# Layer 0: the last two output tiles, the norm and the MLP's first contraction pair by token halves

## The chip, the cores and the metric

The kernel runs on one core of a Trainium2 chip. The metric is the device time of one execution in microseconds; the time before is the median of three runs. Engines are named as in the profile: PE is TensorE's matmuls and PEld its weight loads, DVE is VectorE, ACT ScalarE, POOL GpSimd, and SP the queue that issues the DMAs.

## What is computed

A trunk of two layers on 256 tokens of width 2048, in float32. The part that matters here, for each layer:

```python
mod = cond @ w_ada[l] + b_ada[l]
sh_a, sc_a, g_a, sh_m, sc_m, g_m = [m[:, None, :] for m in jnp.split(mod, 6, axis=-1)]
...
mix = jnp.concatenate([out_a, out_b], axis=-1) @ w_o[l]
x = x + g_a * mix

h = _rmsnorm(x) * (1.0 + sc_m) + sh_m
y = jnp.square(jax.nn.relu(h @ w_mlp_in[l])) @ w_mlp_out[l]
x = x + g_m * y
```

The norm needs the mean square over all 2048 features of a token, so it can't start for a token before the last output tile has been added to x for that token.

## The kernel before

Everything lies transposed: x is 16 tiles of 128 features (partitions) by 256 tokens. Each weight matrix is loaded as float32 (`raw`, five buffers that the modulation weights share) and split into two parts in a rounded format, `hi` by ScalarE (line 146) and `lo` by VectorE (line 147); four buffers of half a weight each hold hi, four hold lo. `mac` multiplies hi by the high part of the activations, hi by the low part, and lo by the high part: three TensorE passes (lines 182 to 184), each with a weight load of its own.

The attention's output product makes two tiles at a time. `pair` calls `tile_cols` for two weights, 16 feature tiles deep, so 48 passes for each tile; `update` (line 1006) adds the result times the gate to x, and `sumsq` squares it. The last two tiles (14 and 15) are squared apart (`sqa`, line 508). Then `rstd` takes the mean with a product in plain float32 (`pn`, line 526), a square root on ScalarE and a reciprocal on VectorE.

`norm_then_by_k` walks over eight pairs of feature tiles, pair 0 to 7. For each, `modulated` makes the two activations: ht on VectorE (line 604), the high part h on ScalarE (605), the low part on VectorE (606). `by_k` splits two weights of 128x1536 and runs 36 passes on each, 72 for a pair, into six PSUM banks (`pk`) that are open over all eight pairs. With these 12 tiles of the MLP begun, `mlp` goes on.

The modulation `mod` is made on VectorE: the weights w_ada come in loads of 1 MB (`ada`, issued on SP at line 289), and one instruction each multiplies by the condition and sums (line 297). There are 192 of them, in the order of need; shift and scale of the MLP come interleaved, four loads for two feature tiles of both. Two things set when a load is issued. Each weight that is split adds `rate` to a credit, and every full credit issues one load:

```python
self.credit += self.rate
while self.credit >= 1.0 and self.ada_todo:
    self.credit -= 1.0
    self.ada_load()
```

And `ada_need(l, g, i)` issues and sums at once, in a row, all that is still missing up to that column, before the work that follows. The rate is 1.1 for a weight in layer 0's output product (`RATE_A0`) and 0.6 in the pairs (`RATE_K`).

The engines' orders are fixed when the program is built. A scheduler sets them, except for PE where `manual_schedule` keeps the order of the code; in layer 0's output product and pairs that is not in force.

Of the kernel before, what the change touches and what calls it, by code (L numbers as in the profile page):

```python
# [10 lines left out]
F32 = mybir.dt.float32  # L11
F32R = mybir.dt.float32r
I32 = mybir.dt.int32
AF = mybir.ActivationFunctionType
ALU = mybir.AluOpType
AX = mybir.AxisListType

P = 128
T = 256
TX = T + 2  # L20
D = 2048
NK = D // P
# [72 lines left out]
NAHEAD = 6  # L95
NNORM = 12


RATE_A0, RATE_A1, RATE_A2, RATE_K, RATE_M = 1.1, 0.5, 0.7, 0.6, 0.66
# [3 lines left out]
class Trunk:  # L103
# [524 lines left out]
            out += self.split(t, "lat")  # L628
        return out

    def norm_then_by_k(self, l, acc, sh, sc, src, n, nwhole, fill=(), early=()):


        r = self.rstd(acc, D) if l or sh else acc
        banks = self.open_banks(2 * n)
        h = []
        for p in range(8):
            k = 2 * p
            for g in (sh, sc):
                self.ada_need(l, g, k + 1)  # L640
            whole = [] if p < nwhole else None
            h += self.modulated(r, k, self.mod[l, sh], self.mod[l, sc], whole)
            self.by_k(banks, [src[l, p, b] for b in range(2)], h, k, NK, 2 * n, whole)
            if fill:
                fill.pop(0)()
            if p in early:
                for g in (sh, sc):
                    self.ada_need(l, g, k + 3)
                early[p](h)
        return h, banks  # L650


    def layer(self, l, acc, st):
        nc, io = self.nc, self.io
# [4 lines left out]
        def next_by_k(kqs):  # L659
            def f(h):  # L660
                if not later:
                    later.extend(self.open_banks(2))
                for kq in kqs:
                    self.by_k(later, [io["w_d"][l, kq]], h, 4 * kq, NK)
            return f

        if l == 0:
            early = {p: next_by_k(kqs) for p, kqs in EARLY.items()}
            h, banks = self.norm_then_by_k(l, acc, 0, 1, io["w_a"], 3, WHOLE, self.fills(), early)
# [3 lines left out]
        else:  # L673
            h = acc
            lat = []
            for b in range(0, NAHEAD, 2):
                t, c = self.scaled(st, b, self.u("cr"))
# [7 lines left out]
        kk, qn, kn, qr, vm, a, at, v, o = [], [], [], [], [], [], [], [], []  # L685
# [108 lines left out]
        acc = None  # L794
        g = self.mod[l, 2]
        self.ada_need(l, 2, NK - 1)
        banks = self.open_banks(2)
# [6 lines left out]
        o = self.mo + o  # L804
        for kq in (2, 3):
            self.by_k(banks, [io["w_oa"][l, kq]], o, 4 * kq, NK)
        st = self.ahead(l, 3, 4, io["w_m0"][0]) if l else None
        for m in range(0, 4, 2):
            self.update(m, banks[m // 2], g)
            acc = self.sumsq(acc, self.x[:, m : m + 2])  # L810
        with self.tc.manual_schedule(engines={mybir.EngineType.PE}) if l else nullcontext():
            for m in range(4, NK, 2):
                self.update(m, self.pair([io["w_ob"][l, m - 4 + j] for j in range(2)], o), g)
                acc = self.sumsq(acc, self.x[:, m : m + 2], l == 0 and m == NK - 2)
                if st:
                    self.ahead_fill(st, 2 if m > 4 else 6)
            self.rate = RATE_K
            if st:
                h = self.ahead_rest(st, 0, acc, 2)
                first = NAHEAD, lambda: [self.relu2(*self.scaled(st, b, self.t("sum"))) for b in range(0, NAHEAD, 2)]  # L820
            else:
                h, banks = self.norm_then_by_k(l, acc, 3, 4, io["w_n0"], 3, 0)
                first = NNORM, lambda: [self.relu2(b) for b in banks]
        self.rate = RATE_M
        with self.tc.manual_schedule(engines={mybir.EngineType.PE}):
            return self.mlp(l, h, first, self.mod[l, 5])
# [437 lines left out]
```

## Time and profile before

| | |
|---|---|
| median of 3 runs | 2213.0 us (2212.81 to 2214.16) |
| profiled execution, its own time | 2214.89 us |
| its span | 2213.1 us |
| PE busy | 2167.0 us, 98% |
| DVE busy | 1613.2 us, 73% |
| ACT busy | 1158.8 us, 52% |
| sums of the modulation (line 297) | 192, 437.5 us |
| mean granted clock of TensorE | 0.991 |

A stretch of the profile reads: from and to, its length, the busy time of PE, PEld, DVE, ACT and POOL with their instructions, the granted clock, the DMA engines' share and GB/s. A row of the timeline has the start, the length, engine, line, tiles and shape; in brackets stands how long the engine had been idle and what released it. Lengths of matmuls overlap: the distance of two starts is what a pass takes from the engine. A waits row gives the sum, the number and the longest.

### The profile page before, as it was taken

How to read it: one execution, taken by the hardware profiler on the slowest of the kernel's cores; microseconds unless marked ns; L12 is line 12 of the kernel's file. 1: busy time of each engine (PE TensorE's matmuls, PEld its weight loads, DVE VectorE, ACT ScalarE, POOL GpSimd, SP SyncE). 2: the span in 40 equal slices, each digit the busy share in tenths (PEclk: the TensorE clock that was granted, in tenths of full speed). 3: DMA queues.
4: the chain of work that ended last, by engine and by line, in shares of the span. 5: the costliest groups of instructions: out<-in, count | busy, mean ns of one | idle time of the engine just before them, and what ended most of it. 6: DMA issues, size and time to landing. Idle time of an engine off the chain costs nothing.

```text
span 2213.1 us, 30961 instructions
## 1 busy us (share of the span) xinstructions
PE 2167.0 (98%) x12290; PEld 1907.8 (86%) x12290; DVE 1613.2 (73%) x2131; ACT 1158.8 (52%) x1722; POOL 25.5 (1%) x43
## 2 busy tenths in 40 slices
PE   7999999899999999999999999999999999999998
PEld 5898889898888888888888898999888888888886
DVE  8989778878778778777799876788544545555566
ACT  6555564446465355345455565647545534544544
POOL 0000000000000000000001000001000000000000
PEclk9999999999999999999999999999999999999999
DMA  9987678798888888888877766675554555555552
GB/s 391 404 332 298 241 276 320 283 339 335 308 318 327 311 307 321 330 307 303 339 253 293 259 243 228 235 287 202 197 198 176 204 195 174 190 207 183 188 202 94
DMA packets 85829, 586.44 MB, mean 265 GB/s; under 512 B 9522, under 2 KB 9906, under 8 KB 19634
## 3 DMA queue, kind: packets, MB, share of 16 engines
q1 hardware_dynamic: 85682, 584.46, 70.6%
q8 instruction: 96, 1.57, 0.3%
q14 instruction: 51, 0.41, 0.1%
HBM read 582.32 MB, written 2.10 MB: 264 GB/s over the span
## 4 chain that ended last, share of the span: by engine, by line
PE 90%; DVE 7%; ACT 2%; issue 1%; DMA 0%; SPq 0%; DVEq 0%; ACTq 0%
PE ps L203 21%; PE ps L206 11%; PE py L976 10%; PE py L974 10%; PE py L978 10%; DVE ada L297 4%; PE ps L184 2%; PE ps L182 2%; PE ps L183 2%; PE pk L184 2%; PE pk L182 2%; PE pk L183 2%; PE pv L253 1%; PE pv L254 1%; PE pv L255 1%; DVE lo L147 1%
## 5 line engine op out<-in xcount | busy, mean ns | idle before, releaser
L147 DVE TENSOR_TENSOR lo<-raw,hi 128x1024 fp32r<-128x1024 f32 (+1 forms) x720 | 850.8, 1194 | 480.4 <-ACT hi L146 322.5
L146 ACT ACTIVATE hi<-raw 128x1024 fp32r<-128x1024 f32 (+1 forms) x720 | 742.1, 1036 | 688.2 <-PE py L978 368.2
L203 PE MATMUL ps<-h,hi 128*128 128x512 f32 x2016 | 472.9, 391 | 0.0
L203 PEld LDWEIGHTS ps<-h,hi 128*128 128x128 f32 x2016 | 375.1, 188 | 75.8 <-DVE h L606 0.2
L297 DVE SCALAR_TENSOR_TENSOR ada<-ada,cond 128x2048 f32<-128x2048 f32 x192 | 437.5, 2284 | 0.7 <-DMA ada<-in_w_ada 0.5
L974 PE MATMUL py<-hi,hid 128*128 128x512 f32 x1024 | 326.5, 390 | 0.0
L976 PE MATMUL py<-lo,hid 128*128 128x512 f32 x1024 | 326.0, 389 | 0.0
L978 PE MATMUL py<-hi,hid 128*128 128x512 f32 x1024 | 325.7, 389 | 0.0
L206 PEld LDWEIGHTS ps<-h,lo 128*128 128x128 f32 x2016 | 250.5, 192 | 5.0
L206 PE MATMUL ps<-h,lo 128*128 128x256 f32 x2016 | 252.0, 283 | 0.0
L976 PEld LDWEIGHTS py<-lo,hid 128*128 128x128 f32 x1024 | 192.2, 188 | 40.7 <-DVE lo L147 0.7
L978 PEld LDWEIGHTS py<-hi,hid 128*128 128x128 f32 x1024 | 192.2, 188 | 40.0
L974 PEld LDWEIGHTS py<-hi,hid 128*128 128x128 f32 x1024 | 191.3, 188 | 38.8
L1012 ACT ACTIVATE sum<-ps 128x256 f32<-128x256 f32 x110 | 42.1, 383 | 110.4 <-PE ps L206 110.3
L182 PE MATMUL pk<-h,hi 128*128 128x256 f32 x304 | 87.8, 291 | 8.8 <-ACT h L605 5.8
L184 PE MATMUL pk<-h,lo 128*128 128x256 f32 x304 | 87.4, 289 | 1.1 <-DVE lo L147 1.1
L183 PE MATMUL pk<-h,hi 128*128 128x256 f32 x304 | 87.7, 289 | 0.0
L176 DVE TENSOR_TENSOR hid<-relu,hid 128x256 fp32r<-128x256 f32 x128 | 48.3, 420 | 47.5 <-ACT hid L175 47.5
L239 PE MATMUL pk<-hf,w 128*128 128x256 f32 x288 | 64.8, 385 | 9.0 <-ACT hf L610 8.9
L239 PEld LDWEIGHTS pk<-hf,w 128*128 128x128 f32 x288 | 55.5, 194 | 17.6 <-ACT hf L610 9.8
L182 PEld LDWEIGHTS pk<-h,hi 128*128 128x128 f32 x304 | 60.0, 198 | 9.9 <-ACT h L605 6.2
L184 PEld LDWEIGHTS pk<-h,lo 128*128 128x128 f32 x304 | 60.0, 198 | 1.5 <-DVE lo L147 1.5
(252 smaller groups left out, 2815.8 us busy)
## 6 DMA issues: line engine op xcount, KB each, us to landing
raw<-in_w_m SPq DMA_DIRECT2D x238, 1024.0 KB, 4.9
ada<-in_w_ada SPq DMA_DIRECT2D x192, 1024.0 KB, 5.0
raw<-in_w_ob SPq DMA_DIRECT2D x24, 1024.0 KB, 4.9
raw<-in_w_dv SPq DMA_DIRECT2D x16, 1024.0 KB, 4.8
raw<-in_w_q SPq DMA_DIRECT2D x16, 1024.0 KB, 5.0
raw<-in_w_n SPq DMA_DIRECT2D x16, 768.0 KB, 5.7
w<-in_w_a SPq DMA_DIRECT2D x24, 384.0 KB, 11.1
raw<-in_w_a SPq DMA_DIRECT2D x12, 768.0 KB, 6.4
```

The source lines that it names most:

```text
L146: nc.scalar.activation(hi, v, AF.Copy)
L147: ins = nc.vector.tensor_tensor(lo, v, hi.bitcast(F32), ALU.subtract)
L182: mm(ps, hi, x[0], start=first, stop=False, skip_group_check=shared)
L183: mm(ps, hi, x[1], start=False, stop=False, skip_group_check=shared)
L184: mm(ps, lo, x[0], start=False, stop=last, skip_group_check=shared)
L203: mm(ps.rearrange("p a b -> p (a b)"), part(w, 0, k), both, start=k == 0, stop=False)
L206: mm(ps[:, 0], part(w, 1, k), x, start=False, stop=k == nk - 1)
L239: self.nc.tensor.matmul(ps, w[i][:, j * P : j * P + P], whole[i], start=first, stop=last, skip_group_check=True)
L297: ins = nc.vector.scalar_tensor_tensor(w, w, 1.0, self.cond, ALU.mult, ALU.mult, accum_out=acc[:, i : i + 1])
L974: mm(o, xh[:, tok], hi[:, part[j]], start=start, stop=False)
L976: mm(o, xh[:, tok], lo[:, part[j]], start=False, stop=False)
L978: mm(o, xl[:, tok], hi[:, part[j]], start=False, stop=stop)
```

## The change

For layer 0 alone, output tiles 14 and 15, the norm and pair 0 are written out in `by_halves`, and PE keeps the order of the code there. Each product is made for tokens 0 to 127 and for tokens 128 to 255 apart, so the passes are 128 columns wide and there are twice as many, each with its weight load. The order on PE is: tile 14 first half, tile 15 first half, tile 14 second half, the mean of the first half, tile 15 second half, pair 0's first weight on the first half, the mean of the second half, the second weight on the first half, both weights on the second half. The updates, squares, root, reciprocal and h are made by halves too. From the weights of tile 12 on, the rate is 0, so that no modulation load is issued on credit until pair 1, where it is 0.6 again. Layer 1's code is only written in another order.

```diff
+    def by_halves(self, l, o, g, acc):
+        nc, io = self.nc, self.io
+        m = NK - 2
+        toks = [slice(t * P, t * P + P) for t in range(2)]
+        sh, sc = self.mod[l, 3], self.mod[l, 4]
+        for grp in (3, 4):
+            self.ada_need(l, grp, 1)
+        ps, pn = self.bank("ps"), self.bank("pn")[:, 0]
...
+        def out(j, tok):
+            for k in range(NK):
+                x = (o[k][0][:, tok], o[k][1][:, tok])
+                self.mac(ps[:, j, tok], ws[j][k // 8], (k % 8) * P, P, x, k == 0, k == NK - 1)
+
+        def squares(tok):
+            for i in range(2):
+                x = self.x[:, m + i, tok]
+                nc.vector.scalar_tensor_tensor(x, ps[:, i, tok], g[:, m + i : m + i + 1], x, ALU.mult, ALU.add)
+            sq = self.t("sqh")[:, :, :P]
+            nc.scalar.activation(sq, self.x[:, m : m + 2, tok], AF.Square)
+            return sq
+
+        def norm(sq, tok):
+            vals = [acc[0][:, tok], acc[1][:, tok], sq[:, 0], sq[:, 1]]
+            for i, v in enumerate(vals):
+                nc.tensor.matmul(pn[:, tok], self.mean[D], v, start=i == 0, stop=i == 3)
...
+        out(0, toks[0])
+        out(1, toks[0])
+        sq = squares(toks[0])
+        out(0, toks[1])
+        norm(sq, toks[0])
+        out(1, toks[1])
+        sq = squares(toks[1])
+        banks = self.open_banks(6)
...
+        into(0, toks[0])
+        norm(sq, toks[1])
+        into(1, toks[0])
+        into(0, toks[1])
+        into(1, toks[1])
+        return r, banks, h
...
-        for p in range(8):
+        for p in range(len(h) // 2, 8):
...
+        if l == 0:
+            for m in range(4, NK - 2, 2):
+                if m == NK - 4:
+                    self.rate = 0.0
+                self.update(m, self.pair([io["w_ob"][l, m - 4 + j] for j in range(2)], o), g)
+                acc = self.sumsq(acc, self.x[:, m : m + 2])
+            with self.tc.manual_schedule(engines={mybir.EngineType.PE}):
+                begun = self.by_halves(l, o, g, acc)
+            self.rate = RATE_K
+            h, banks = self.norm_then_by_k(l, None, 3, 4, io["w_n0"], 3, 0, begun=begun)
```

What that does to the built order shows at three places. First PE, at the end of the output product (ps is its PSUM bank, pn the mean's, pk the pair's; in brackets the engines whose semaphores the row waits for). Before:

```order
L183 MATMUL ps_3841<-do_3052,hi_3910 128x256
L184 MATMUL ps_3841<-do_3052,lo_3911 128x256
L526 MATMUL pn_3971<-sqa_3967,mean_117 128x256 [waits Activation_49]
L526 MATMUL pn_3971<-sqa_3969,mean_117 128x256 [waits Activation_49]
L182 MATMUL pk_3979<-h_3986,hi_3996 128x256 [waits Activation_49]
L182 MATMUL pk_3980<-h_3986,hi_3996 128x256
L182 MATMUL pk_3981<-h_3986,hi_3996 128x256
L183 MATMUL pk_3979<-h_3986,hi_3996 128x256 [waits DVE_49]
```

and now, where tile 15 of the first half is done and tile 14 of the second half begins:

```order
L183 MATMUL ps_3838<-do_3052,hi_3857 128x128
L184 MATMUL ps_3838<-do_3052,lo_3858 128x128
L182 MATMUL ps_3838<-moh_2463,hi_3843 128x128 [waits DVE_49]
L183 MATMUL ps_3838<-mol_2464,hi_3843 128x128
L184 MATMUL ps_3838<-moh_2463,lo_3844 128x128
L182 MATMUL ps_3838<-moh_2463,hi_3843 128x128
L183 MATMUL ps_3838<-mol_2464,hi_3843 128x128
L184 MATMUL ps_3838<-moh_2463,lo_3844 128x128
```

The wide passes with two waits for ScalarE's squares and one for h between them became narrow ones; the first pass of the second half waits for VectorE, for the update of x that reads the same bank.

Second the DMA queue, from pair 4's second weight on (raw is a weight, in_w_n a pair's and in_w_m the MLP's; ada is a modulation load). Before:

```order
L158 DMA raw_4465<-in_w_n 128x1536
L158 DMA raw_4522<-in_w_n 128x1536
L289 DMA ada_4532<-in_w_ada 128x2048
L158 DMA raw_4570<-in_w_n 128x1536
L158 DMA raw_4626<-in_w_n 128x1536
L289 DMA ada_4636<-in_w_ada 128x2048
L158 DMA raw_4674<-in_w_n 128x1536
L289 DMA ada_4686<-in_w_ada 128x2048
L158 DMA raw_4733<-in_w_n 128x1536
L158 DMA raw_4780<-in_w_n 128x1536
L289 DMA ada_4790<-in_w_ada 128x2048
L158 DMA raw_4832<-in_w_m 128x2048
```

and now, behind pair 5's second weight:

```order
L289 DMA ada_4746<-in_w_ada 128x2048
L289 DMA ada_4786<-in_w_ada 128x2048
L289 DMA ada_4789<-in_w_ada 128x2048
L158 DMA raw_4802<-in_w_n 128x1536
L158 DMA raw_4848<-in_w_n 128x1536
L289 DMA ada_4858<-in_w_ada 128x2048
L289 DMA ada_4897<-in_w_ada 128x2048
L289 DMA ada_4901<-in_w_ada 128x2048
L289 DMA ada_4904<-in_w_ada 128x2048
L158 DMA raw_4917<-in_w_n 128x1536
L289 DMA ada_4927<-in_w_ada 128x2048
L158 DMA raw_4965<-in_w_n 128x1536
```

Where single loads stood between the weights, three stand ahead of pair 6's two weights and four ahead of pair 7's first.

Third VectorE ahead of pair 7's h (macc and mod are the modulation's sums and results; ht and h are pair 7's). Before:

```order
L147 TENSOR_TENSOR lo_4677<-raw_4674,hi_4676 128x768
L147 TENSOR_TENSOR lo_4681<-raw_4674,hi_4680 128x768
L297 SCALAR_TENSOR_TENSOR ada_4636,macc_88<-ada_4636,cond 128x2048
L147 TENSOR_TENSOR lo_4736<-raw_4733,hi_4735 128x768
L307 SCALAR_TENSOR_TENSOR mod_87<-macc_88,vec 128x2
L604 SCALAR_TENSOR_TENSOR ht_4724<-x,mod_87,rstd_3976 128x256 x2
L147 TENSOR_TENSOR lo_4740<-raw_4733,hi_4739 128x768
L606 SCALAR_TENSOR_TENSOR h_4725<-ht_4724,mod_85,h_4725 128x256
L606 SCALAR_TENSOR_TENSOR h_4726<-ht_4724,mod_85,h_4726 128x256
```

and now:

```order
L147 TENSOR_TENSOR lo_4855<-raw_4848,hi_4854 128x768
L297 SCALAR_TENSOR_TENSOR ada_4858,macc_86<-ada_4858,cond 128x2048
L297 SCALAR_TENSOR_TENSOR ada_4897,macc_86<-ada_4897,cond 128x2048
L297 SCALAR_TENSOR_TENSOR ada_4901,macc_88<-ada_4901,cond 128x2048
L309 TENSOR_TENSOR mod_85<-macc_86,vec 128x2
L297 SCALAR_TENSOR_TENSOR ada_4904,macc_88<-ada_4904,cond 128x2048
L307 SCALAR_TENSOR_TENSOR mod_87<-macc_88,vec 128x2
L604 SCALAR_TENSOR_TENSOR ht_4908<-x,mod_87,rstd_3840 128x256 x2
L147 TENSOR_TENSOR lo_4920<-raw_4917,hi_4919 128x768
L606 SCALAR_TENSOR_TENSOR h_4909<-ht_4908,mod_85,h_4909 128x256
```

Four sums stand in a row between the last split of pair 6 and pair 7's ht, where one sum stood among the splits; ahead of pair 6's ht three sums stand in the same way.

More of the change, by code (lines that the diff above doesn't have):

```diff
@@ L629, in latent, with into @@
         return out
[L631 to L636, printed above, removed]
-        for p in range(8):
+    def by_halves(self, l, o, g, acc):
[6 more added lines that the diff above has]
+        ps, pn = self.bank("ps"), self.bank("pn")[:, 0]
+        r = self.cp.tile([P, T], F32, tag="rstd", name=self.name("rstd"), bufs=2)
+        ws = [self.weights(io["w_ob"][l, m - 4 + j]) for j in range(2)]
+        h = [self.parts("h") for _ in range(2)]
+        def out(j, tok):
[13 more added lines that the diff above has]
+                nc.tensor.matmul(pn[:, tok], self.mean[D], v, start=i == 0, stop=i == 3)
+            nc.scalar.activation(r[:, tok], pn[:, tok], AF.Sqrt, bias=self.eps)
+            nc.vector.reciprocal(r[:, tok], r[:, tok])
+            t = self.t("hth")
+            for i, (hi, lo, _) in enumerate(h):
+                nc.vector.scalar_tensor_tensor(t[:, i, tok], self.x[:, i, tok], sc[:, i : i + 1], r[:, tok], ALU.mult, ALU.mult)
+                nc.scalar.activation(hi[:, tok], t[:, i, tok], AF.Identity, bias=sh[:, i : i + 1])
+                nc.vector.scalar_tensor_tensor(
+                    lo[:, tok], t[:, i, tok], sh[:, i : i + 1], hi[:, tok].bitcast(F32), ALU.add, ALU.subtract
+                )
+        out(0, toks[0])
[6 more added lines that the diff above has]
+        banks = self.open_banks(6)
+        w = []
+        def into(b, tok):
+            for i, part in enumerate(w[b]):
+                for j in range(6):
+                    tile = 6 * b + j
+                    x = (h[i][0][:, tok], h[i][1][:, tok])
+                    first = i == 0 and tile % 2 == 0 and tok.start == 0
+                    self.mac(banks[tile // 2][:, tile % 2, tok], part, j * P, P, x, first, False, True)
+        for b in range(2):
+            w.append(self.weights(io["w_n0"][l, 0, b], 1536))
+        into(0, toks[0])
[4 more added lines that the diff above has]
+        return r, banks, h
@@ L638, in norm_then_by_k @@
+    def norm_then_by_k(self, l, acc, sh, sc, src, n, nwhole, fill=(), early=(), begun=None):
+        if begun:
+            r, banks, h = begun
+        else:
+            r, banks, h = acc, self.open_banks(2 * n), []
+        for p in range(len(h) // 2, 8):
             k = 2 * p
@@ L810, in layer @@
             acc = self.sumsq(acc, self.x[:, m : m + 2])
-        with self.tc.manual_schedule(engines={mybir.EngineType.PE}) if l else nullcontext():
-            for m in range(4, NK, 2):
+        if l == 0:
+            for m in range(4, NK - 2, 2):
+                if m == NK - 4:
+                    self.rate = 0.0
                 self.update(m, self.pair([io["w_ob"][l, m - 4 + j] for j in range(2)], o), g)
-                acc = self.sumsq(acc, self.x[:, m : m + 2], l == 0 and m == NK - 2)
-                if st:
+                acc = self.sumsq(acc, self.x[:, m : m + 2])
[3 more added lines that the diff above has]
+            h, banks = self.norm_then_by_k(l, None, 3, 4, io["w_n0"], 3, 0, begun=begun)
+            first = NNORM, lambda: [self.relu2(b) for b in banks]
+        else:
+            with self.tc.manual_schedule(engines={mybir.EngineType.PE}):
+                for m in range(4, NK, 2):
+                    self.update(m, self.pair([io["w_ob"][l, m - 4 + j] for j in range(2)], o), g)
+                    acc = self.sumsq(acc, self.x[:, m : m + 2])
                     self.ahead_fill(st, 2 if m > 4 else 6)
-            self.rate = RATE_K
-            if st:
+                self.rate = RATE_K
                 h = self.ahead_rest(st, 0, acc, 2)
[L820 to L823, printed above, removed]
+            first = NAHEAD, lambda: [self.relu2(*self.scaled(st, b, self.t("sum"))) for b in range(0, NAHEAD, 2)]
         self.rate = RATE_M
```

## The prediction

> **What bounds the kernel now.** I read the busy shares and the chain that ended last first, then stretches of ten microseconds around the changed place, then the waits of TensorE there.
>
> ```profile
> PE 2167.0 (98%) x12290; PEld 1907.8 (86%) x12290; DVE 1613.2 (73%) x2131; ACT 1158.8 (52%) x1722; POOL 25.5 (1%) x43
> PE 90%; DVE 7%; ACT 2%; issue 1%; DMA 0%; SPq 0%; DVEq 0%; ACTq 0%
> ...
> 410.00:420.00 10.00, 8.95 (x72) 8.64 (x70) 9.96 (x12) 1.64 (x3) 0.00 (x0) 1.00 0.86 323
> 420.00:430.00 10.00, 2.85 (x11) 2.04 (x11) 9.16 (x17) 3.97 (x8) 0.00 (x0) 0.68 0.89 308
> 430.00:440.00 10.00, 10.00 (x71) 10.00 (x71) 9.26 (x20) 6.47 (x13) 0.00 (x0) 0.80 0.33 120
> 440.00:450.00 10.00, 10.00 (x86) 10.00 (x85) 9.55 (x12) 4.00 (x5) 0.00 (x0) 1.00 0.77 277
> 490.00:500.00 10.00, 10.00 (x86) 10.00 (x85) 8.22 (x9) 7.34 (x14) 0.00 (x0) 1.00 1.00 378
> ...
> PE pk L182 <- ACT h L605: 5.8, 1, 5.8
> PE pn L526 <- ACT sqa L508: 2.4, 2, 2.0
> ```
>
> TensorE (the first busy number of a stretch) bounds nearly everything; from 440 us on it has no gap until the pairs end at 500. The seam between the output product and the MLP's first pair is the exception: two waits there sum to 8.2 us, and the granted clock (third number from the right) falls to 0.68 and 0.80. The seam pass by pass:
>
> ```profile
> 406.42 0.28 PE L182 MATMUL ps<-moh,hi 128*128 128x256 f32 x1
> ...
> 418.55 0.28 PE L183 MATMUL ps<-do,hi 128*128 128x256 f32 x1
> 418.67 0.28 PE L184 MATMUL ps<-do,lo 128*128 128x256 f32 x1
> 420.98 0.70 PE L526 MATMUL pn<-sqa,mean 128*128 128x256 f32 x2 [2.02 <-ACT sqa L508]
> 422.01 0.70 PE L526 MATMUL pn<-sqa,mean 128*128 128x256 f32 x2 [0.34 <-ACT sqa L508]
> 428.55 1.01 PE L182 MATMUL pk<-h,hi 128*128 128x256 f32 x3 [5.84 <-ACT h L605]
> 429.36 0.41 PE L183 MATMUL pk<-h,hi 128*128 128x256 f32 x1
> 429.57 0.41 PE L184 MATMUL pk<-h,lo 128*128 128x256 f32 x1
> ...
> 439.63 0.28 PE L182 MATMUL pk<-h,hi 128*128 128x256 f32 x1
> ```
>
> The first row opens output tile 14, the last opens contraction pair 1. So what the change rewrites takes 439.63 - 406.42 = 33.2 us now, for 96 + 72 = 168 passes. A pass of 256 tokens starts every 0.12 us at full clock (418.55 to 418.67) and every 0.21 us just after the gap (429.36 to 429.57). All the change can win lies in these 33.2 us: 168 x 0.12 = 20.2 is work, 8.2 waits, and the rest half clock and the norm's own products.
>
> **The change part by part.**
>
> *Half as wide, twice as many.* The 168 passes become 336 of 128 tokens, each with its own weight load. What does a 128-token pass cost? The trace has no such pass in this number format; the nearest rows:
>
> ```profile
> 500.27 7.28 PE ps L203 x32
> 507.55 3.83 PE ps L206 x32
> ...
> 40.15 0.28 PE L375 MATMUL pl<-vec,mean 128*128 128x4 f32 x2
> ...
> 40.15 0.19 PEld L375 LDWEIGHTS pl<-vec,mean 128*128 128x128 f32 x1
> 40.26 0.19 PEld L453 LDWEIGHTS pb<-oh,lsch 128*128 128x128 f32 x1
> 40.38 0.19 PEld L454 LDWEIGHTS pb<-oh,lscl 128*128 128x128 f32 x1
> ...
> 97.52 0.19 PEld L182 LDWEIGHTS pk<-h,hi 128*128 128x128 f32 x1 [0.99 <-ACT hi L146]
> 97.63 0.19 PEld L183 LDWEIGHTS pk<-h,hi 128*128 128x128 f32 x1
> ...
> 222.49 0.60 PE L1094 MATMUL pt<-ident,a 128*128 128x128 f32 x4
> ```
>
> The chain gives 7.28 / 32 = 0.2275 us for 512 columns and 3.83 / 32 = 0.12 for 256; along that line 128 columns would be 0.12 - 0.054 = 0.066. But a load stands before each pass. At 40.15 the passes have four columns, next to nothing, and still loads start 0.11 and 0.12 apart. At 97.52, after a wait, the second load starts 0.11 after the first. [...] I take 0.112, nearest the four-column rows; ends: 0.066, if short loads overlap better than any row shows, and 0.12. Then 336 x 0.112 = 37.6 us.
>
> [...]
>
> *The norm's products.* Four plain float32 matmuls, which the trace records as eight passes of 256 columns, become eight, so 16 passes of 128. The four transposes in the last row, of that width and format, start (0.60 - 0.28) / 3 = 0.11 apart, 0.28 being the length of one pass: 1.8 us.
>
> *A new wait.* The first pass of the second token half writes the PSUM bank that VectorE still reads for the residual update of the first half, and the built order makes it wait for that.
>
> ```profile
> 406.62 0.88 DVE L1006 SCALAR_TENSOR_TENSOR x<-ps,mod,x 128x256 f32<-128x256 f32 x2 [2.15 <-PE ps L184]
> 416.04 1.82 DVE L147 TENSOR_TENSOR lo<-raw,hi 128x768 fp32r<-128x768 f32 x2
> 423.60 1.75 DVE L533 RECIPROCAL rstd<-rstd 128x256 f32<-128x256 f32 x1
> 425.26 2.23 DVE L297 SCALAR_TENSOR_TENSOR ada<-ada,cond 128x2048 f32<-128x2048 f32 x1
> 427.42 1.27 DVE L604 SCALAR_TENSOR_TENSOR ht<-x,mod,rstd 128x256 f32<-128x256 f32 x3
> 428.61 1.27 DVE L606 SCALAR_TENSOR_TENSOR h<-ht,mod,h 128x256 fp32r<-128x256 f32 x3
> ...
> 412.93 1.58 ACT L146 ACTIVATE hi<-raw 128x768 fp32r<-128x768 f32 x2 [2.88 <-DMA raw<-in_w_n]
> ```
>
> Two updates of half width lie between 0.45 and 0.88 us; with the end of the last pass (0.28, less one pitch) and the hand-over I take 0.9. Behind it queue all later passes. The rest of the norm is covered: after the half's mean product, split 0.9, reciprocal 0.9 (half of 1.75), four half-width steps and two on ScalarE make some 3.5 us, against 48 x 0.112 = 5.4 us of the other tile; the second half's some 3 us lie beside 36 x 0.112 = 4.0. If a pass took 0.066, that second cover (2.4) would be gone.
>
> So the stretch becomes 37.6 + 1.8 + 0.9 = 40.3 us instead of 33.2: **+7.1**. The 8.2 us of waits and the half clock do go; the loads eat more than that. Ends: +6.5 at 0.110, +9.8 at 0.12, -8.3 at 0.066.
>
> *The postponed modulation loads.* Five load-and-sum steps move from the seam behind it. On SP they leave slots to the weights; nothing there is scarce, since PE never waits for a DMA in this stretch. But pair p needs columns 2p and 2p+1 of scale and shift, four sums, and the rate gives 1.2 per pair. Before, the lead sufficed to pair 7. Now it runs out: in VectorE's order three sums stand in a row ahead of pair 6's h and four ahead of pair 7's, where one stood in each place. No sum is added in all, but here they are on the path. From the rows: a sum 2.2 (425.26 to 427.42), a split of a half weight 0.91, an ht or h step 0.40, a split on ScalarE 0.79; a pair on TensorE 72 x 0.12 = 8.6.
>
> VectorE can split pair 4's last half weight when TensorE leaves pair 3, since the buffers hold four halves. From the start of pair 4: 1.8 for both engines' splits and their hand-over, 2.2 sum, 0.9, 0.8, 0.9, 0.8 for pair 5's splits and h, 2.2 sum: 9.6, which is 1.0 after pair 5 began. Then two splits (2.8), three sums (9.4), three splits, two ht and an h (13.3). Pair 5 ends at 8.6: TensorE waits **4.7 us**. Then an h, a split, four sums, two ht, a split, an h: 12.2 more, at 25.5; pair 6 ended at 13.3 + 8.6 = 21.9: **3.6 us**. Together 8.2 (25.5 against two pairs).
>
> Such waits also cost clock:
>
> ```profile
> 208.60:211.30 2.70, 0.00 (x0) 0.00 (x0) 1.96 (x10) 2.04 (x5) 0.00 (x0) 1.00 0.91 373
> 212.10:218.90 6.80, 6.23 (x26) 5.43 (x25) 5.83 (x13) 3.57 (x9) 0.00 (x0) 0.50 0.45 172
> ...
> 1161.10:1164.00 2.90, 0.02 (x1) 0.03 (x1) 2.90 (x7) 2.17 (x5) 0.74 (x2) 1.00 0.33 136
> 1164.40:1167.80 3.40, 3.40 (x18) 3.40 (x17) 3.40 (x6) 0.46 (x1) 0.00 (x0) 0.50 0.60 169
> ```
>
> Waits of 2.7 and 2.9 us brought half clock for 6.8 and 3.4 us. At 0.21 instead of 0.12, 3.4 us at half clock lose 1.5 us. The loss after the first wait is hidden, since pair 7 starts when VectorE lets it; after the second it is 1.5 to 3.0, and I take 2. So **+10.2**; ends 5 (some sums finish while the half weights are still in hand) and 14 (loads land late too: DMA stood at 0.77 to 1.00 of its time in pairs 1 to 7, and seven 1 MB loads now crowd into two pairs).
>
> Sum: 7.1 + 10.2 = 17.3. Against the profiled execution's own 2214.9 that is 2232.2; the median of the three runs stands 1.9 lower, so I forecast 2213.0 + 17.3, rounded to **2230 us**.
>
> **The rivals.**
> - *A short pass is priced by its columns* (0.066). For: the two chain rows lie on a line. Against: loads 0.11 apart under four-column passes. The stretch shrinks by 8.3, the forced sums stay: 2213.0 - 8.3 + 10.2 = 2214.9, not slower within what a measurement can tell. It decides below 0.074 per pass (30.5 - 10.2 + 4.4 over 336); below 0.06 the kernel would be faster. [...] Chance 0.13.
> - *The forced sums stay hidden*: VectorE takes them while it waits for weight slots. For: it is only 73% busy in all. Against: its order is fixed, and its stretches here are 8 to 9.6 us busy of 10. Then 2213.0 + 7.1 = 2220. Chance 0.08.
> - *Narrow passes lose the fast format* and run like plain float32, whose 128-column records take 0.11, two to a matmul: 0.22. Then 336 x 0.22 = 73.9, the stretch grows by 43, and the time is about 2266. Nothing in the trace shows it. Chance 0.06.
>
> **How the numbers follow.** The forecast case has 0.67; its own range is 2225 to 2236 (passes 0.110 to 0.12, sums 6 to 13). The rivals have 0.27, and 0.06 is left for what I don't see, half of it faster. A measurement of this kernel tells about 0.2%, 4.4 us, from no change. Faster: 0.02 of the first rival and 0.03, 0.05. Same: 0.06 of the first rival and 0.01, 0.07. Slower: 0.88. The range 2216 to 2238 takes in the second rival and the slower half of the first, and leaves out the third, the fast half and the tails.
>
> **What would show it.** In the profile after: the starts of 128-token passes 0.11 to 0.12 apart, with a load interval as long; no wait of PE for h or sqa left; one wait of about 0.9 us for the residual update; two waits of TensorE of 3 to 5 us ahead of pairs 6 and 7, with sums just before on VectorE, and half clock behind each. The prediction is wrong if passes start 0.07 apart, or if no wait stands ahead of pairs 6 and 7.

## Result: 27 us slower, ten more than forecast

| kernel | median, us | runs | ratio to before, 95% interval |
|---|---|---|---|
| before | 2213.3 (2212.8 to 2214.2) | 4 | |
| after | 2240.5 (2237.1 to 2244.6) | 4 | 1.0123 [1.0111, 1.0135] |

The sign was right; the time lies 10.5 us above the forecast of 2230 and 2.5 us above the range. The four executions fall in two groups, 2244.6 and 2243.8, and 2237.1 and 2237.3. The profiled one is that of 2244.6 us (span 2242.8; before 2214.9 and 2213.1), so the trace has 29.7 us to explain. Where passes open, in after less before:

| place in TensorE's order | after, us | later than before, us |
|---|---|---|
| output tile 14 | 406.36 | -0.1 |
| contraction pair 1 | 459.55 | 19.9 |
| pair 5 | 494.14 | 20.0 |
| pair 6 | 506.61 | 23.8 |
| pair 7 | 519.17 | 27.7 |
| the MLP's second product | 551.23 | 28.9 |
| end | 2242.81 | 29.7 |

Twenty microseconds are lost in the rewritten seam, 9.0 more from pair 1 to the second product, 0.8 in layer 1. In pairs 1 to 4 nothing is lost: the 9.0 begin with the wait ahead of pair 6.

The rewritten seam in stretches; the granted clock is the third number from the right, DMA's share the second:

```profile
406.40:412.00 5.60, 5.60 (x53) 5.60 (x52) 2.70 (x4) 1.61 (x2) 0.00 (x0) 1.00 0.52 180
420.40:430.00 9.60, 9.60 (x47) 9.60 (x47) 3.44 (x5) 2.18 (x4) 0.00 (x0) 0.50 0.10 26
430.00:440.00 10.00, 10.00 (x49) 10.00 (x49) 3.21 (x7) 2.62 (x5) 0.00 (x0) 0.50 0.13 53
440.00:447.60 7.60, 7.60 (x38) 7.60 (x37) 0.00 (x0) 0.00 (x0) 0.00 (x0) 0.50 0.42 140
447.70:455.00 7.30, 7.30 (x68) 7.30 (x67) 6.90 (x18) 4.07 (x10) 0.00 (x0) 1.00 0.00 0
```

TensorE has work throughout: busy time fills every stretch. But it does 53 passes in 5.6 us in the first, and 49 in 10 us in the third, where the clock is 0.50. The half clock lasts from 420.35 to 447.65, 27.3 us. Its passes, its beginning and its end:

```profile
416.81 0.28 PE L183 MATMUL ps<-do,hi 128*128 128x128 f32 x1
416.92 0.28 PE L184 MATMUL ps<-do,lo 128*128 128x128 f32 x1
417.89 0.33 PE L182 MATMUL ps<-moh,hi 128*128 128x128 f32 x1 [0.70 <-DVE x L652]
418.06 0.28 PE L183 MATMUL ps<-mol,hi 128*128 128x128 f32 x1
...
425.56 0.41 PE L183 MATMUL ps<-do,hi 128*128 128x128 f32 x1
425.77 0.41 PE L184 MATMUL ps<-do,lo 128*128 128x128 f32 x1
425.99 1.16 PE L660 MATMUL pn<-acc,mean 128*128 128x128 f32 x4
...
448.05 0.27 PE L184 MATMUL pk<-h,lo 128*128 128x128 f32 x1
448.16 0.27 PE L182 MATMUL pk<-h,hi 128*128 128x128 f32 x1
```

At full clock a narrow pass starts every 0.11 us (416.81 to 416.92, and again at 448.05), at half clock every 0.21 (425.56 to 425.77). The only idle time of TensorE in the whole seam is the 0.70 us ahead of 417.89, the wait for VectorE's residual update; the clock falls 2.5 us behind it. It comes back only after the second set of norm products (pn).

TensorE's waits in the whole trace, those that changed (line, releaser: us in total, times, longest):

```profile
PE pa L184 <- DVE lo L147: 6.0, 3, 4.9
PE pk L182 <- ACT h L605: 4.7, 2, 3.7
PE ps L182 <- DVE x L652: 0.7, 1, 0.7
```

The first row was 4.3 us before, its longest 2.9; it stands at the start of layer 1, where the last 0.8 us are lost. The waits for h and sqa in the seam are gone (5.8 and 2.4 us before). The two for h that are left stand ahead of pairs 6 and 7, and half clock follows the first of them only (505.68 to 512.51):

```profile
506.61 0.80 PE L182 MATMUL pk<-h,hi 128*128 128x256 f32 x2 [3.66 <-ACT h L605]
...
519.17 0.62 PE L182 MATMUL pk<-h,hi 128*128 128x256 f32 x3 [1.08 <-ACT h L605]
```

And the loads' place in the DMA engines, from stretches of 20 us, before and then after:

```profile
420.00:440.00 20.00, 12.85 (x80) 12.04 (x81) 18.43 (x36) 10.44 (x21) 0.00 (x0) 0.74 0.61 214
```

```profile
420.00:440.00 20.00, 20.00 (x98) 20.00 (x97) 6.65 (x11) 4.80 (x8) 0.00 (x0) 0.51 0.12 40
...
500.00:520.00 20.00, 15.05 (x100) 14.44 (x98) 19.93 (x28) 6.30 (x10) 0.00 (x0) 0.83 1.01 395
```

What was transferred at 0.61 of DMA's time in the seam is transferred at pairs 6 and 7, where DMA stands at 1.01, that is, all of its time.

### The profile page after: what moved, and what is told of

It reads as the page before. It is cut to its first block, busy times and chain, and to the rows that moved or that the text cites. A ratio compares the mean times of both kernels' runs of the same rounds, so it can differ in the third digit from the quotient of the medians.

```text
span 2242.8 us, 31313 instructions
## 1 busy us (share of the span) xinstructions
PE 2197.7 (98%) x12466; PEld 1940.2 (87%) x12466; DVE 1613.4 (72%) x2138; ACT 1160.8 (52%) x1725; POOL 22.6 (1%) x43
## 4 chain that ended last, share of the span: by engine, by line
PE 78%; DVE 3%; issue 0%; ACT 0%; DVEq 0%; ACTq 0%
PE ps L203 20%; PE ps L206 11%; PE py L1051 10%; PE py L1053 10%; PE py L1049 10%; PE ps L182 1%; PE ps L184 1%; PE ps L183 1%; PE pk L183 1%; PE pk L184 1%; PE pk L182 1%; PE pa L184 1%; PE pa L183 1%; PE pa L182 1%; DVE ada L297 1%; PE pv L255 1%
## 5 line engine op out<-in xcount | busy, mean ns | idle before, releaser
L182 PE MATMUL pk<-h,hi 128*128 128x256 f32 (+1 forms) x328 | 95.7, 296 | 7.7 <-ACT h L605 4.7
L184 PE MATMUL pk<-h,lo 128*128 128x256 f32 (+1 forms) x328 | 95.4, 293 | 1.1 <-DVE lo L147 1.1
L183 PE MATMUL pk<-h,hi 128*128 128x256 f32 (+1 forms) x328 | 95.7, 293 | 0.5 <-DVE h L606 0.5
L182 PEld LDWEIGHTS pk<-h,hi 128*128 128x128 f32 x328 | 66.4, 205 | 8.7 <-ACT h L605 5.1
L184 PEld LDWEIGHTS pk<-h,lo 128*128 128x128 f32 x328 | 66.2, 203 | 1.5 <-DVE lo L147 1.5
```

Source lines behind the costliest of these rows:

```text
L182: mm(ps, hi, x[0], start=first, stop=False, skip_group_check=shared)
L183: mm(ps, hi, x[1], start=False, stop=False, skip_group_check=shared)
L184: mm(ps, lo, x[0], start=False, stop=last, skip_group_check=shared)
```

## Experiments

Every run compares with the kernel before on the same chip, whose medians were 2213.1 to 2214.0 us.

| run | what differs | median, us | ratio, 95% interval |
|---|---|---|---|
| e0 | after again | 2236.8 | one run |
| e1 | after, loads at rate 1.0 | 2236.5 | 1.0116 [1.0076, 1.0155] |
| e2 | before, loads moved | 2219.5 | 1.0026 [1.0017, 1.0036] |
| e3 | after, two banks | 2228.7 | 1.0068 [1.0053, 1.0083] |
| e4 | after, loads back | 2237.2 | 1.0123 [1.0090, 1.0155] |
| e5 | e3, loads at rate 1.1 | 2233.3 | 1.0088 [1.0074, 1.0102] |
| e6 | before, fewer loads moved, rate 1.0 | 2217.5 | 1.0016 [1.0007, 1.0025] |
| e8 | e4 with two banks | 2222.6 to 2241.6 | 1.0090 [1.0059, 1.0121] |
| e9 | e3, wait of 0.70 us put back | 2236.9 | 1.0127 [1.0090, 1.0163] |
| e10 | e5, short sums | 2229.9 | 1.0073 [1.0059, 1.0087] |
| e11 | e3, short sums | 2229.4 | 1.0071 [1.0057, 1.0085] |
| e12 | before, two sums later | 2210.3 | 0.9986 [0.9976, 0.9995] |
| e13 | e3, wait of 0.44 us | 2240.6 | 1.0121 [1.0102, 1.0140] |
| e14 | e11, short loads too | 2221.3 | 1.0035 [1.0023, 1.0048] |

### The clock: is it the wait?

**e3, two banks.** One PSUM bank for each token half, so the first pass of the second half has nothing to wait for:

```diff
-        ps, pn = self.bank("ps"), self.bank("pn")[:, 0]
+        pss, pn = {0: self.bank("ps"), P: self.bank("ps")}, self.bank("pn")[:, 0]
...
-                self.mac(ps[:, j, tok], ws[j][k // 8], (k % 8) * P, P, x, k == 0, k == NK - 1)
+                self.mac(pss[tok.start][:, j, tok], ws[j][k // 8], (k % 8) * P, P, x, k == 0, k == NK - 1)
```

> The changed kernel, with a PSUM bank of its own for each token half of the two output tiles, so that the first pass of the second half no longer waits for VectorE's residual update (0.7 us at 417.2). Rows of three and four sums stay. Theory A1 (the wait tips TensorE into half clock, and the narrow passes alone keep full clock): no half clock between 417 and 448, 13 us and the wait less, 2224 to 2231. Theory A2 (narrow passes bring half clock by themselves after some ten microseconds, wait or none): the half-clock stretch stays at about the same place, 2236 to 2244.

2228.7 us (2228.4 to 2229.3). The seam of e3, in stretches:

```profile
404.80:416.00 11.20, 11.20 (x103) 11.20 (x102) 3.04 (x6) 1.61 (x2) 0.00 (x0) 1.00 0.35 126
416.00:430.00 14.00, 14.00 (x128) 14.00 (x127) 6.84 (x13) 5.06 (x9) 0.00 (x0) 1.00 0.17 57
430.00:444.00 14.00, 14.00 (x128) 14.00 (x127) 10.90 (x24) 7.31 (x14) 0.00 (x0) 1.00 0.22 76
```

The same narrow passes hold full clock for 39 us. The stretch from tile 14 to pair 1 is 39.3 us, 6.1 over before. A wait of 0.7 us was worth some 13 us: A1, not A2.

**e9, the wait put back.** But e3 also changes the banks. So one product of four columns that reads the updated tile 15 goes ahead of the second half:

```diff
+        spare = self.bank("spare")
+        nc.tensor.matmul(spare[:, 0, :4], self.mean[D], self.x[:, m + 1, :4], start=True, stop=True)
         out(0, toks[1])
```

> The two-bank form of the changed kernel (2228.7 us), with one product of four columns that reads the updated residual, put ahead of the second token half of tile 14: it brings the wait for VectorE's update back, while the token halves keep banks of their own. The only work added is that product. Theory A (the wait tips the clock): half clock comes back behind it and lasts through the narrow passes, 2237 to 2245. Rival (two halves in one bank slow TensorE or its clock, the wait is incidental): full clock, 2229 to 2231.

2258.0, 2237.1, 2236.8 and 2235.9 us, where 2237 to 2245 was expected. The profiled one is the first:

```profile
417.23 0.39 PE L675 MATMUL spare<-x,mean 128*128 128x4 f32 x2 [0.70 <-DVE x L652]
```

```profile
450.00:470.20 20.20, 20.20 (x96) 20.20 (x96) 9.39 (x20) 6.58 (x12) 0.00 (x0) 0.50 0.12 39
470.30:474.10 3.80, 3.80 (x19) 3.80 (x19) 0.96 (x1) 0.84 (x1) 0.00 (x0) 0.50 0.24 45
474.30:480.60 6.30, 6.30 (x55) 6.30 (x54) 4.26 (x5) 2.46 (x3) 0.00 (x0) 1.00 0.38 135
```

With the wait the half clock is back, this time for 54.6 us: through all the narrow passes and 4 us into pair 1, which opens at 470.25. From 474.3 us on the clock is 1.00. The three executions without a trace have a mean granted clock of 0.988 to 0.989, and all four of e3 have 0.992: that is 14 to 18 us more of half clock, worth 6 to 9 us (at 0.476, worked out at e0 below), and their times are 7 to 8 us above e3's. So the wait is the cause, not the shared bank.

**e0, the changed kernel again.** 

> The changed kernel as it is, for a second trace of it. Its runs lay in two groups, 2237 and 2244 us. [...] Expected: a time between 2231 and 2252, and a half-clock stretch between 417 and 460 whose length explains it to within 2 us. Rival: the stretch is as long and the difference lies elsewhere.

2236.8 us. The half clock now lasts 10.2 us; it ends behind the first set of norm products instead of the second:

```profile
418.60:428.60 10.00, 10.00 (x49) 10.00 (x48) 2.25 (x3) 2.05 (x3) 0.00 (x0) 0.50 0.01 2
428.80:450.40 21.60, 21.60 (x195) 21.60 (x195) 15.12 (x33) 10.00 (x19) 0.00 (x0) 1.00 0.23 85
```

17.1 us less of half clock at 1 - 0.112 / 0.213 = 0.476 are 8.1 us. The stretch to pair 1 is 45.1 us instead of 53.2, shorter by 8.1. The span is 7.8 shorter, so the two traces differ by the length of the half clock. The executions without a trace fit: the mean granted clock is 0.985 in the two near 2244 us and 0.989 in the three near 2237, which is 18 us of half clock or 8.6 us of time (0.001 of the clock is 4.5 us of half clock, so this is known to some 2 us).

**e13, a shorter wait.** The product of e9 reads tile 14, which VectorE updates first: `self.x[:, m, :4]`.

> As the run that brought the wait back (two banks and a four-column product), but the product reads the tile whose update VectorE finishes first, so that TensorE waits about 0.3 us instead of 0.7. [...] Rival (any wait in a narrow stretch tips it): 2236 to 2245, or up to 2258.

2240.6 us (2236.3 to 2244.9): the rival's time came.

```profile
415.77 0.28 PE L184 MATMUL ps<-do,lo 128*128 128x128 f32 x1
416.49 0.38 PE L675 MATMUL spare<-x,mean 128*128 128x4 f32 x2 [0.44 <-DVE x L652]
...
418.40:428.50 10.10, 10.10 (x49) 10.10 (x49) 2.44 (x3) 2.05 (x3) 0.00 (x0) 0.50 0.01 3
```

The wait was 0.44 us, not 0.3; from pass start to next start it is 0.72 us (415.77 to 416.49), of which the last pass's own record takes 0.28. Half clock is back, for 10.1 us: 0.44 us was enough here, and a wait of 0.3 us was not tested.

**What the traces tell of the waits.** TensorE's short waits among the narrow passes of the seam, and the clock behind each:

| trace | wait, us | for | half clock behind it, us |
|---|---|---|---|
| after | 0.70 | update of x | 27.3 |
| e0 | 0.7 | update of x | 10.2 |
| e4 | 0.70 | update of x | 30.7 |
| e9 | 0.70 | update of x | 54.6 |
| e13 | 0.44 | update of x | 10.1 |
| e4 | 0.72 | a split of weights | none |
| e8 | 0.72 | a split of weights | none |
| e3 | no wait | | none |

The length of the wait does not sort them: behind 0.72 us the clock stayed at 1.00 twice, behind 0.44 us it fell to 0.50. What tells them apart is not shown, nor why half clock lasts 10.2 us in one execution of the changed kernel and 27.3 in another.

### The loads

**e2, wide passes with only the loads moved.**

```diff
             for m in range(4, NK, 2):
+                if l == 0 and m == NK - 4:
+                    self.rate = 0.0
...
-            self.rate = RATE_K
+            self.rate = RATE_K if l else 0.0
...
             self.by_k(banks, [src[l, p, b] for b in range(2)], h, k, NK, 2 * n, whole)
+            if sh:
+                self.rate = RATE_K
```

> The kernel before, its passes 256 tokens wide, with only the modulation loads moved: none from output tile 12 to pair 0, then 0.6 of the rate, so that the rows of three and four sums stand ahead of pairs 6 and 7 as in the changed kernel. Theory A: two sums of 2.2 us leave VectorE's path in the seam, so that the wait of 5.8 us ahead of pair 0 falls to about 1.5 (-4.4); the forced sums cost 8.6; about 2217, and up to 4 us less if the shorter wait also spares half clock. Rival B: only the gain, about 2209. If the time is 2213 + 17 or more, the loads and not the narrow passes carry the loss.

2219.5 us (2218.0 to 2220.6). The wait ahead of pair 0 fell from 5.84 to 3.47 us and the seam by 4.8 us; pairs 6 and 7 and the first output pass then came 4.6, 3.9 and 2.3 us later, 10.9 in all. Waits for h in e2, three in place of one:

```profile
PE pk L182 <- ACT h L605: 9.7, 3, 4.5
```

**e4, the narrow passes with the loads back.** `self.rate = 0.0` is taken out, and the rates of before put in its place.

> The changed kernel with its token halves, but with the modulation loads left in the seam at the rates of the kernel before, so that no rows of sums stand ahead of pairs 6 and 7. Theory A: pairs 6 and 7 give back 8.6 us; sums of 2.2 us stand within the halves' norm on VectorE, whose cover was 5.4 and 4.0 us beside some 3.5 us of norm, so waits of 0 to 4 us come back; half clock in the narrow passes stays; 2230 to 2240. Rival B: 2237 or more.

2237.2 us. From pair 1 to the second product nothing is lost (21.0 us late at both), so all 9.0 us are the moved loads'. The median says nothing of it, since half clock lasts 30.7 us in this trace: against e0's 10.2 that is 9.8 us of time, and the two times (2236.4 and 2236.8) are level; against after's 27.3 it is 1.6, and after's trace is 8.2 us longer.

**e8, e4 with two banks.** 

> Token halves with two banks, and the modulation loads left in the seam as in the kernel before: the halves alone, with neither the wait for the update nor the moved loads. Theory A (halves cost 6.1 us at full clock, the moved loads the other 8.6 and some later): 2219 to 2222, as long as no other short wait comes up in the narrow stretch; a wait of 0.7 us for a split of weights stood there in the one-bank form, and if it stays it may bring half clock, then 2232 or more. Rival B (the loads cost nothing where they stand): 2228.

2223.5, 2222.6, 2241.4, 2241.6 and 2239.1 us. The profiled execution is the first. There TensorE waits 0.72 us for a split, and the clock holds:

```profile
412.73 0.33 PE L184 MATMUL ps<-moh,lo 128*128 128x128 f32 x1 [0.72 <-DVE lo L147]
...
406.30:420.00 13.70, 12.98 (x117) 12.84 (x116) 10.07 (x13) 2.95 (x4) 0.00 (x0) 1.00 0.80 295
420.00:434.00 14.00, 14.00 (x127) 14.00 (x127) 10.07 (x15) 4.64 (x8) 0.00 (x0) 1.00 0.42 142
434.00:446.50 12.50, 12.50 (x114) 12.50 (x114) 11.60 (x28) 7.72 (x16) 0.00 (x0) 1.00 0.34 136
```

The stretch is 40.2 us, 7.0 over before, with one short wait in it. The same wait for a split, 0.72 us, stands in e4's trace at 411.25 us, and there too the clock is 1.00 from 404.8 to 417.8 us; behind the update's wait at 417.31, 0.70 us, it is 0.50 from 417.9 on. So both runs count against "any wait tips it". The other executions of e8 have no trace, but the granted clock is 0.992 in the two near 2223 us and 0.984 to 0.986 in the three near 2240: 27 to 36 us more of half clock, or 13 to 17 us of the 16 to 19 that part them. Which wait brought it is not shown.

**e1 and e5, the loads spread.** One word in each: the rate behind the halves is 1.0 (e1, on after) or 1.1 (e5, on e3) instead of 0.6.

> The changed kernel, but the load-and-sum steps return at 1.0 instead of 0.6 of the planner's rate from pair 1 on, so that no three or four of them stand in a row ahead of pairs 6 and 7. Theory A (the narrow passes in the seam lose 13 us to half clock, the forced sums cost what pairs 6 and 7 grew by, 8.6 us): the waits of 3.7 and 1.6 us ahead of pairs 6 and 7 go, the half-clock stretch in the seam stays, time about 8.6 us under the changed kernel, 2229 to 2236. Rival B (the forced sums are hidden, what pairs 6 and 7 lose is only a clock that would fall anyway): no change, 2237 to 2245.

2236.5 us, between the two ranges, with executions from 2231.5 to 2252.5 (granted clocks 0.991 and 0.981). In the trace 6.1 us are lost from pair 1 to the second product, against 9.0 in after, so spreading gave back 2.9 where 8.6 was expected. The wait ahead of pair 6 is gone, one of 4.2 us ahead of pair 7 is there instead.

> The two-bank form with the load-and-sum steps at 1.1 instead of 0.6 of the rate in pairs 1 to 7: no row of more than two sums is left. Token halves cost 6.1 us there (stretch 39.3 instead of 33.2, measured in the two-bank form), no half clock in the narrow passes. Theory A: the rest (8.6 and 1.6 us later) goes but for the two or three microseconds by which VectorE is short in pairs 1 to 7 (12 sums of 2.28, 28 splits of 0.91, 24 steps of 0.40, 62.5 us against 60.5): 2219 to 2223. Rival B: sums cost nothing however they stand, 2227 to 2229.

2233.3 us: a miss, and dearer than the rows of sums. Full clock in the seam; then 13.6 us are lost from pair 1 to the second product, against 9.0 in e3. ScalarE's waits there point to late weights (in e3 the same row has 9.3 us in 4 waits):

```profile
ACT hi L146 <- DMA raw<-in_w_n: 27.2, 8, 5.9
```

**e10 and e11, short sums.** Each sum behind the seam over 256 of 2048 columns, the loads whole:

```diff
-                w, w, 1.0, self.cond, ALU.mult, ALU.mult, accum_out=acc[:, i : i + 1]
+                w[:, : self.cut], w[:, : self.cut], 1.0, self.cond[:, : self.cut], ALU.mult, ALU.mult, accum_out=acc[:, i : i + 1]
```

> The two-bank form with the loads spread over pairs 1 to 7 (2233.3 us), but each modulation sum in those pairs over 256 of its 2048 columns: the loads stay whole, VectorE's 2.28 us a sum become some 0.4, and the sums are not the reference's there. Theory C (what the spread loads cost is transfer time: DMA stood at 0.95 to 0.99 there and ScalarE waited 27 us for weights): weights still land late, 2229 to 2234. Theory D (VectorE's time): the waits behind pair 1 go, 2219 to 2223.

> The two-bank form with its rows of three and four sums (2228.7 us), each of these sums again over 256 of 2048 columns, the loads whole. Theory A, as forecast (VectorE's sums in a row are the path): a row of three takes 1.2 instead of 6.8 us, the waits of 3.7 and 1.6 us ahead of pairs 6 and 7 go, 2219 to 2222. Theory C (the loads' transfers are the path): waits stay within 2 us of what they were, 2225 to 2229.

2229.9 us for e10 and 2229.4 for e11: by the medians, cutting VectorE's share of the loads to a fifth gives 3.4 us back when they are spread, and nothing when they stand in rows. By place, in the profiled executions, 7.5 us are lost from pair 1 to the second product in both, so 6.1 of e5's 13.6 and 1.5 of e3's 9.0 came back. In e11 TensorE no longer waits ahead of pair 6, and ahead of pair 7 it waits 3.46 us for a weight that ScalarE splits, not for h. The row of sums there says why (VectorE, with the idle time before each sum):

```profile
492.49 0.43 DVE L297 SCALAR_TENSOR_TENSOR ada<-ada,cond 128x256 f32<-128x256 f32 x1 [1.74 <-DMA ada<-in_w_ada]
494.99 0.43 DVE L297 SCALAR_TENSOR_TENSOR ada<-ada,cond 128x256 f32<-128x256 f32 x1 [1.87 <-DMA ada<-in_w_ada]
497.73 0.42 DVE L297 SCALAR_TENSOR_TENSOR ada<-ada,cond 128x256 f32<-128x256 f32 x1 [2.31 <-DMA ada<-in_w_ada]
```

A sum takes 0.43 us and the next still starts 2.5 to 2.7 us later, because its load lands then. In after the same row stood back to back:

```profile
497.02 2.28 DVE L297 SCALAR_TENSOR_TENSOR ada<-ada,cond 128x2048 f32<-128x2048 f32 x1
499.23 0.08 DVE L297 DVE_READ_ACCUMULATOR ada<-ada,cond 128x1 f32 x1
499.23 2.29 DVE L297 SCALAR_TENSOR_TENSOR ada<-ada,cond 128x2048 f32<-128x2048 f32 x1
```

One every 2.2 us there. Sums and transfers run at nearly one pace, and taking away the sums' time left the transfers': from 480 to 500 us DMA stands at 0.9 of its time or more in every slice of 1.9 us in e11. The reverse, short transfers under whole sums, was not tried.

**e14, short loads too.** As many issues and buffers, an eighth of the bytes:

```diff
-        self.nc.sync.dma_start(w, self.io["w_ada"][l, NK * g + i])
+        self.nc.sync.dma_start(w[:, : self.cut], self.io["w_ada"][l, NK * g + i][:, : self.cut])
```

> The two-bank form with sums over 256 columns behind the seam (2229.4 us), and now the loads cut to those 256 columns as well: as many issues and buffers, an eighth of the bytes; the sums are not the reference's there. Theory C (bytes: the moved loads compete with the weights): no weight lands late from pair 1 to the first output pass, 2219 to 2222. Rival (the issues or the five shared buffers are what is short): 2227 to 2230.

2221.3 us (2220.8 to 2221.7). From pair 1 to the second product nothing is lost (4.2 us late at both). So it is the bytes, not the number of issues. A short load may also give its buffer back sooner, and no run parts the two; that DMA had hardly any time left there in e11 speaks for the transfers. DMA from 440 to 500 us, e11 and then e14:

```profile
440.00:500.00 60.00, 57.16 (x480) 56.95 (x478) 35.16 (x72) 23.86 (x34) 0.00 (x0) 1.00 0.83 321
```

```profile
440.00:500.00 60.00, 60.00 (x504) 60.00 (x504) 38.59 (x76) 28.24 (x38) 0.00 (x0) 1.00 0.66 225
```

**e6 and e12, the gain alone.** What e2 won in the seam, without its price? e6 stops the loads two tiles later (`m == NK - 2`) and goes on at 1.0 from pair 1.

> The kernel before with wide passes; loads stop only from output tile 14's weights to pair 0, so that the two sums that stood on the seam's path are moved, and go on at 1.0 from pair 1, one sum between any two splits. Theory A: the seam gains the 4.9 us that it gained in the wide kernel without loads; VectorE, which stood at 0.80 to 0.96 in pairs 1 to 7, has about as much room as the two or three sums more need (4.5 to 6.8 us): waits of 0 to 3 us. 2208 to 2211. Rival B (VectorE has no room and waits of over 2 us bring half clock again): 2213 to 2217.

2217.5 us, where 2208 to 2211 was expected: the seam gains 4.6 us and all is lost again from pair 7 to the second product. The weights are late at the first output pass, with DMA at 0.99 from 440 us on:

```profile
498.05 9.36 PE L203 MATMUL ps<-h,hi 128*128 128x512 f32 x32 [1.81 <-ACT hi L146]
...
440.00:500.00 60.00, 57.02 (x459) 55.84 (x459) 56.09 (x72) 29.62 (x49) 0.00 (x0) 0.99 0.99 383
```

e12 leaves every load's issue where the rates of before put it, and only holds back the two sums:

```diff
-        self.ada_sums(ins)
+        None if self.hold else self.ada_sums(ins)
...
+            self.hold = sh == 3 and p == 0
             self.by_k(banks, [src[l, p, b] for b in range(2)], h, k, NK, 2 * n, whole)
+            self.hold = False
```

> The kernel before with wide passes and with every load where it was; only the two sums that stood on VectorE in front of pair 0's h are put behind pair 0, so that the transfers still use the seam, where DMA was at 0.6 of its time. Theory C (transfers were what made moved loads dear): the seam gains its 4 to 5 us, and VectorE has room for two sums later: 2207 to 2210. Theory D (VectorE is short behind the seam whatever the transfers do): the gain is lost again by the first output pass, 2212 to 2215.

2210.3 us (2209.2 to 2211.1, 11 runs), ratio 0.9986 [0.9976, 0.9995]: 3.2 us under before and 30 under after. That is less than the 0.2% of the prediction's bound, though the interval of these eleven runs lies wholly below 1. TensorE's wait ahead of pair 0, and the two sums behind pair 0's last steps on VectorE:

```profile
423.68 1.43 PE L182 MATMUL pk<-h,hi 128*128 128x256 f32 x5 [4.15 <-ACT h L605]
...
431.85 2.28 DVE L297 SCALAR_TENSOR_TENSOR ada<-ada,cond 128x2048 f32<-128x2048 f32 x1
434.06 2.29 DVE L297 SCALAR_TENSOR_TENSOR ada<-ada,cond 128x2048 f32<-128x2048 f32 x1
```

The wait ahead of pair 0 is 1.7 us shorter, the one for the squares 1.3 (2.4 to 1.0), and half clock lasts 6.8 us instead of 10.2. The stretch to pair 1 shrinks by 4.0 us and nothing is given back: it is 5.6 us early at pair 1 and at the second product, 1.6 of which it had at tile 14, ahead of what was changed. VectorE had room for the sums (52.77 us busy of the 60 from 440 us on); DMA had none for the loads (0.99 of its time in e6).

## Why the prediction was right and wrong

- **A narrow pass at 0.112 us: right.** 0.111 to 0.112 wherever the clock was full. The 0.066 of the columns is out, as is float32's 0.22.
- **The new wait of 0.9 us: right in place and size, wrong in what it does.** TensorE idles for 0.70 us, and with the end of the last pass it is 0.86 (416.92 to 417.89, less one pitch of 0.11). I priced what queues behind it and not the clock.
- **The stretch, +7.1: the step that failed.** It costed all 336 passes at full clock. At full clock it was right: 7.0 in e8 with one short wait, 6.1 in e3 with none. In after's trace it measured +20.0, of which 27.3 x 0.476 = 13.0 are half clock; in e0 +11.9, of which 10.2 x 0.476 = 4.9. "The 8.2 us of waits and the half clock do go" held for the waits alone. Half clock behind waits was in the working, behind 2.7 and 2.9 us: I read those as long waits and did not ask what a short one does among narrow passes. The cases I left 0.06 for included this one; it stood in both traces of after, and the granted clocks of all five executions fit one of its two lengths. My signs of being wrong did not reach it: passes did start 0.11 us apart wherever the clock was full, waits did stand ahead of pairs 6 and 7, and a pitch of 0.21 us was not among the signs.
- **The moved loads, +10.2: the size about right, the mechanism half right.** Measured from pair 1 to the second product: 9.0 in after and e3, 10.2 in e0, 11.2 in e2. The waits stood ahead of pairs 6 and 7 with sums in a row (3.7 and 1.1 us, and 0.5 more for pair 7's low part, against 4.7 and 3.6). Half clock stood behind the first alone in after, behind both in e0. Its loss behind the first is hidden, as I wrote: that stretch is 6.8 us in after and 3.4 in e0, and pair 7 opens 12.56 us after pair 6 in both. Behind the second it was nothing in after and 1.2 us in e0, where I took 2. But I wrote that nothing on SP's side is scarce since TensorE never waits for a DMA. e11 and e14 show that bytes were the equal bound: by place short sums gave back 1.5 of the 9.0 us, short loads the other 7.5. Late loads stood in the forecast only as the upper end of its range. That the size fits is in part luck: a load lands every 2.5 to 2.7 us and a sum takes 2.2, so either bound gives nearly one price. In the seam of before DMA had 0.39 of its time free, from 440 to 500 us 0.09.
- **Forced sums hidden (rival, 0.08): no.** e2 and e4 show the price of the moved steps; what of it is the sums alone is the 1.5 us of e11.
- **Sum.** In after's trace 7.0 for the stretch at full clock, 13.0 of half clock, 9.0 for the loads and 0.8 in layer 1 are 29.8 us, of 29.7; in e0's 7.0, 4.9, 10.2 and 0.9 are 23.0, of 21.9 at the end and 1.1 that it was early at tile 14. The forecast had 17.3 because it lacked the second term. e3, without that term and without the wait, ran in 2228.7 us; the forecast less its 0.9 for the wait is 2229.4.

## What to carry to other kernels

Before halving a pass, price what a short wait among the narrow passes may do to the clock, beside what queues behind it: here waits of 0.44 and 0.70 us were followed by 10 to 55 us at half clock, and two of 0.72 us by none. Then either leave no wait at all in such a stretch, with a bank of its own for each half (39 us at full clock in e3), or stay wide. And when work is put off from a gap, move only what the gap lacks: here the sums could go and gain 3 us, while the loads that went with them gave up transfer time that existed only there.

## What was not expected of the hardware

- A wait of 0.70 us was followed by 27.3 us at half clock in after, 10.2 in e0 and 54.6 in e9, and one of 0.44 us by 10.1 in e13; behind waits of 0.72 us in e4 and e8 the clock stayed at 1.00.
- Narrow passes hold either clock: 39 us at full in e3, all but the last 4 of the 54.6 us at half in e9, by one wait of 0.70 us.
- One kernel can have times 19 us apart on one chip (e8, 2222.6 to 2241.6) by how long half clock lasts: shown in the traces for after against e0 (8 us), by the granted clocks for e8 (0.992 to 0.984). What sets the length is not shown.
- Open: what tells a wait that costs the clock from one that does not, and whether one under 0.44 us is safe in a narrow stretch, which no run reached.
